# Head norms in the two mixers on 8 columns, in a four-layer decoder trunk on one core

## The chip, the cores and the metric

One core of a Trainium2 chip. The metric is the device time of one execution in microseconds (us), median of several runs; lower is better. PE is TensorE (PEld its weight loads), DVE VectorE, ACT ScalarE, POOL GpSimd, SP the queue that issues DMAs.

## The reference

The program is a trunk of residual layers on 512 positions of 1024 channels. Each layer is a SwiGLU FFN, a mixer, and another FFN. Layer 0's mixer (mixer A) is a recurrent one with 12 heads of 64 channels, together with a cross-attention of 4 heads to a memory of 256 rows. Layer 1's mixer (mixer B) is a dilated sliding-window attention of 12 heads, with the same kind of memory attention. What matters here are norms over the 64 channels of a head, at each position:

```
kk = split_heads(k * kk_scale)
kk = kk / jnp.maximum(jnp.linalg.norm(kk, axis=-1, keepdims=True), 1e-12)
...
y = ((y - mean) * lax.rsqrt(var + LNX_EPS)).reshape(b, s, RWKV_W) * lnx_g + lnx_b
...
q = rms_norm(q, q_gain)          # queries of the memory and of the dilated attention
k = rms_norm(split_heads(k), k_gain)
logits = jnp.einsum('bshd,bmhd->bhsm', q, k).astype(jnp.float32) / math.sqrt(HEAD_DIM)
```

## The kernel before

Activations lie transposed: 128 channels (two heads, a "pair") on the partitions, 512 positions in the free dimension, eight such tiles for 1024 channels. Products with weights (`dense`, L416) split each f32 operand into a high and a low part and make three matmuls of 512 columns in place of one f32 matmul, which would be slower; the weights' parts are made by ACT (`whi`) and by DVE or POOL (`wlo`), in the mixers by POOL alone. All else on PE is plain f32, in two records for each matmul in the trace, or a transpose by the identity.

Mixer A (`mixer_a`) projects six pairs of recurrent heads and two pairs of memory queries. For each pair `rwkv_prepare` makes the decays, the normed kk and the scaled operands, `rwkv_solve` inverts triangular blocks in steps that alternate between PE and DVE (tiles `tx` and `TT`, 32x32 matmuls), and `rwkv_finish` carries the state through eight chunks and norms the output. Mixer B (`mixer_b`) projects 8 query, 6 key and 6 value tiles; `settle` norms or transposes each, `dilated` makes the attention in 8 units of 128 positions and one pair, and `memory_attention` (used by both mixers) is called for each of the memory's two pairs.

A head's norm (`head_norm`) squares the tile on ACT, sums the squares with one f32 matmul against `same`, a 128x128 matrix of ones in two diagonal blocks, so that each channel of the head holds the sum, takes the root on ACT, inverts 128x512 numbers on DVE in four reciprocals of 128 columns (`invert`), and multiplies tile, gain and inverse on DVE. All 64 rows of a head hold the same number. `rwkv_prepare` and `rwkv_finish` do the same in their own code, with a floor of 1e-12 for kk. There are 28 such norms: in mixer A 6 of kk, 6 of the output and 2 of memory queries, in mixer B 6 of keys and 8 of queries (6 dilated, 2 memory). Four more, of the memory's keys, run on 256 columns in the FFNs.

What sets the order: the mixers are generators ("strands") woven by `weave`, which keeps a planner's clock for each engine (`Meter`) and at each point resumes the first strand in its list whose last result is due; projections come near the end of the list and so fill the gaps. The instructions then stand in that fixed order in each engine's queue. The recording helper is one line, L292, so groups are told apart by tile: `tmp` are work tiles, `krv` a pair's k, r, v, `sc`, `mm`, `py` and `fps` banks of PSUM (`sc` has four), `cst` the constants (`same`, the identity and the masks), `qn` and `kh` queries and keys of mixer B, `prob` its logits, `mpr` the memory's probabilities, `rstd` the layer norm's factor.

## Time and profile before

| | |
|---|---|
| median of three runs | 2133.26 us (2132.96 to 2133.29) |
| profiled execution, its time | 2133.8 us |
| its span | 2131.9 us |
| mean granted PE clock | 0.983 |
| busy | PE 97%, PEld 77%, DVE 46%, ACT 38%, POOL 28% |
| mixer A, about | 385 to 775 us |
| mixer B, about | 1538 to 1773 us |

A row of groups reads: line, engine, operation, out<-in, shapes, count | busy us, mean ns of one | idle time of the engine just before them and what ended most of it. PE's records overlap, so the mean of one matmul is longer than the distance to the next. A row of the chain of waits is a start, a duration in us, an engine and a tile. The clock of a row by stretch is the share of full speed that PE was granted.

### The profile page before, as it was taken

What the parts mean: (1) busy time and instruction counts of PE and PEld (TensorE: products, weight loads), DVE (VectorE), ACT (ScalarE), POOL (GpSimd) and SP (SyncE); (2) the same over time, 40 slices, a digit from 0 to 9 for tenths busy, and PEclk for the clock granted to TensorE, in tenths of its full rate; (3) what the DMA queues carried; (4) which work ended last, traced back from release to release, by engine and by line L of the source; (5) the groups of instructions that cost most, each with busy time, mean ns of one, the idle gap of its engine ahead of it and who ended that gap; (6) DMA issues with size and microseconds to landing.
All of it is one profiled execution on the core that took longest, in us unless ns stands there. A gap on an engine that the chain in (4) does not pass through costs nothing.

```text
span 2131.9 us, 35298 instructions
## 1 busy us (share of the span) xinstructions
PE 2057.6 (97%) x14270; PEld 1642.0 (77%) x14270; DVE 971.3 (46%) x1354; ACT 818.1 (38%) x1418; POOL 593.2 (28%) x514
## 2 busy tenths in 40 slices
PE   8999999979888899999999999999999999999999
PEld 6888888857665678788888888888777667888887
DVE  6333343564748556333434533333367675333322
ACT  6333333423334554333433433333336454333321
POOL 2222222643433143222222222222242224222221
PEclk9999999989999899999999999999999899999999
DMA  5333344411100064363344433334531044323342
GB/s 194 98 95 98 91 136 125 117 46 35 44 23 22 13 216 144 98 183 95 110 124 140 145 97 99 96 102 126 149 109 49 29 159 157 96 97 96 94 136 82
DMA packets 130644, 222.04 MB, mean 104 GB/s; under 512 B 14232, under 2 KB 31824, under 8 KB 130480
## 3 DMA queue, kind: packets, MB, share of 16 engines
q1 hardware_dynamic: 130480, 219.78, 33.6%
q8 instruction: 112, 1.84, 0.4%
q14 instruction: 52, 0.43, 0.1%
HBM read 202.84 MB, written 21.61 MB: 105 GB/s over the span
## 4 chain that ended last, share of the span: by engine, by line
PE 66%; DVE 5%; ACT 1%; POOL 1%; issue 1%; DVEq 0%; POOLq 0%
PE fps L292 51%; PE mm L292 7%; PE sc L292 6%; DVE tmp L292 2%; PE py L292 2%; DVE prob L292 1%; DVE tx L292 0%; DVE mpr L292 0%; DVE x L292 0%; DVE ul L292 0%; DVE krv L292 0%; ACT tmp L292 0%; ACT mpr L292 0%; POOL tmp L292 0%; DVE mx L292 0%
## 5 line engine op out<-in xcount | busy, mean ns | idle before, releaser
L292 POOL TENSOR_TENSOR wlo<-raw,whi 128x512 fp32r<-128x512 f32 (+3 forms) x404 | 495.3, 1227 | 1411.3 <-ACT whi L292 1402.4
L292 ACT ACTIVATE whi<-raw 128x512 fp32r<-128x512 f32 (+3 forms) x684 | 416.0, 610 | 943.3 <-PE fps L292 780.0
L292 PE MATMUL fps<-uh,whi 128*128 128x512 f32 x1408 | 551.4, 392 | 8.7 <-ACT whi L292 8.7
L292 PE MATMUL fps<-uh,wlo 128*128 128x512 f32 x1408 | 549.7, 391 | 2.4 <-DVE wlo L292 2.4
L292 PE MATMUL fps<-ul,whi 128*128 128x512 f32 x1408 | 548.9, 390 | 0.0
L292 DVE TENSOR_TENSOR wlo<-raw,whi 128x512 fp32r<-128x512 f32 x280 | 201.0, 718 | 346.5 <-ACT whi L292 336.9
L292 PEld LDWEIGHTS fps<-uh,whi 128*128 128x128 f32 x1408 | 264.9, 188 | 68.6 <-ACT whi L292 11.9
L292 PEld LDWEIGHTS fps<-uh,wlo 128*128 128x128 f32 x1408 | 264.9, 188 | 59.8 <-DVE wlo L292 4.0
L292 PEld LDWEIGHTS fps<-ul,whi 128*128 128x128 f32 x1408 | 264.9, 188 | 55.4 <-issue 0.7
L292 PE MATMUL fps<-hh,whi 128*128 128x512 f32 x704 | 273.9, 389 | 0.0
L292 PE MATMUL fps<-hl,whi 128*128 128x512 f32 x704 | 273.9, 389 | 0.0
L292 PE MATMUL fps<-hh,wlo 128*128 128x512 f32 x704 | 273.9, 389 | 0.0
L292 DVE TENSOR_TENSOR gs<-fps,rstd 128x512 f32<-128x512 f32 x88 | 60.5, 690 | 322.8 <-PE fps L292 322.8
L292 PEld LDWEIGHTS fps<-hl,whi 128*128 128x128 f32 x704 | 132.1, 188 | 27.5
L292 PEld LDWEIGHTS fps<-hh,whi 128*128 128x128 f32 x704 | 132.1, 188 | 27.4
L292 PEld LDWEIGHTS fps<-hh,wlo 128*128 128x128 f32 x704 | 132.1, 188 | 27.4
L292 PE MATMUL mm<-uh,whi 128*128 128x512 f32 x280 | 123.1, 440 | 0.5 <-DVE p L292 0.2
L292 DVE TENSOR_TENSOR hm<-fps,gs 128x512 f32<-128x512 f32 x88 | 60.6, 691 | 120.3 <-PE fps L292 115.8
L292 PE MATMUL mm<-ul,whi 128*128 128x512 f32 x280 | 115.2, 411 | 0.0
L292 PE MATMUL mm<-uh,wlo 128*128 128x512 f32 x280 | 114.2, 408 | 0.0
L292 DVE RECIPROCAL tmp<-tmp 128x128 f32<-128x128 f32 x112 | 97.2, 916 | 22.5 <-ACT tmp L292 22.1
L292 DVE TENSOR_TENSOR hl<-hm,hh 128x512 fp32r<-128x512 f32 x88 | 77.0, 877 | 51.0 <-ACT hh L292 51.0
(262 smaller groups left out, 2093.5 us busy)
## 6 DMA issues: line engine op xcount, KB each, us to landing
raw<-w SPq DMA_DIRECT2D x512, 256.0 KB, 2.6
raw<-wa_in SPq DMA_DIRECT2D x44, 256.0 KB, 2.7
xd<-x SPq DMA_DIRECT2D x40, 256.0 KB, 3.9
tmp<-xd SPq DMA_DIRECT2D x32, 256.0 KB, 3.6
xin<-xd SPq DMA_DIRECT2D x32, 256.0 KB, 4.2
raw<-w_kv SPq DMA_DIRECT2D x24, 256.0 KB, 2.7
raw<-w SPq DMA_DIRECT2D x32, 128.0 KB, 2.3
raw<-wmem SPq DMA_DIRECT2D x16, 256.0 KB, 2.6
```

What stands on the lines that cost most here:

```text
L292: r = f(*args, **kw)
```

## The change

The sum of squares is now taken by position and head. For each block of 128 positions the squared tile is the stationary side of a matmul, and `pair`, two columns of `same` (one per head), the moving side: positions lie on the partitions, and the four blocks and two heads make 8 columns. Scaling, epsilon (or the floor, now on the square), reciprocal and root run there (`roots`), the reciprocal before the root. Then there are two ways.

- Wide (18 norms: kk, output, keys of mixer B): the root writes each number 64 times, and `spread` multiplies the result with the identity, which brings it back to channels by positions in PSUM, from where the product reads it.
- Narrow (10 norms, all of queries): the tile stays as it is. The factor of a position and head goes into the logits, where positions lie on the partitions: as a scalar in the addition of the bias in `dilated`, and in the maximum and the scale of the exponential in `memory_attention`. The query's gain and 1/8 are folded into the keys' gain, once, at the program's start.

The memory's keys keep the old form (`wide=False`), with the folded gain. The diff, cut to its core:

```diff
+        self.gains = self.cp.tile([P, 3], F32, name="gains")
+        for i, (q, k) in enumerate(GAINS):
+            nc.vector.tensor_scalar(self.gains[:, i:i + 1], self.v(q), self.v(k), 0.125, op0=ALU.mult, op1=ALU.mult)
...
+        self.pair = self.same.rearrange("p (e u) -> p e u", e=2)[:, :, 0]
...
+    def head_rms(self, t, n, tmp, bank, wide=False):
+        sq = tmp()
+        self.nc.scalar.activation(sq, t, AF.Square)
+        yield WAIT
+        return (yield from self.roots(sq, n, bank, tmp if wide else None, 1.0 / HD, EPS, ALU.mult, ALU.add))
+
+    def roots(self, sq, n, bank, wide, *change):
+        nc, nb = self.nc, n // P
+        ps = bank("sc")[:, :nb * 2].rearrange("p (b e) -> p b e", e=2)
+        for b in range(nb):
+            nc.tensor.matmul(ps[:, b], sq[:, b * P:(b + 1) * P], self.pair, start=True, stop=True,
+                             skip_group_check=True)
+        r = self.xp.tile([P, 4, 2], F32, tag="roots", bufs=ROOTS, name=self.nm("roots"))[:, :nb]
+        nc.vector.tensor_scalar(r, ps, *change[:2], **{f"op{i}": o for i, o in enumerate(change[2:])})
+        nc.vector.reciprocal(r, r)
+        yield WAIT
+        if wide:
+            w = wide().rearrange("p (b e u) -> p b e u", e=2, u=HD)
+            nc.scalar.activation(w, r.unsqueeze(3).broadcast_to([P, nb, 2, HD]), AF.Sqrt)
+            r = w.rearrange("p b e u -> p b (e u)")
+        else:
+            nc.scalar.activation(r, r, AF.Sqrt)
+        yield WAIT
+        return r
+
+    def spread(self, r, ps):
+        for b in range(r.shape[1]):
+            self.nc.tensor.matmul(ps[:, b * P:(b + 1) * P], r[:, b], self.ident, start=True, stop=True,
+                                  skip_group_check=True)
...
-            nc.vector.tensor_scalar(mx, mx, -0.125, None, op0=ALU.mult)
+            rh = r[:, 2 * h:2 * h + 2].rearrange("p i e -> p e i")
+            nc.vector.scalar_tensor_tensor(mx, mx, -1.0, rh, op0=ALU.mult, op1=ALU.mult)
...
-                    nc.scalar.activation(pr[e][:, i], lg[e][:, i], AF.Exp, bias=mx[:, e, i:i + 1], scale=0.125,
+                    nc.scalar.activation(pr[e][:, i], lg[e][:, i], AF.Exp, bias=mx[:, e, i:i + 1], scale=rh[:, e, i:i + 1],
...
-        ss = self.bank("sc")
-        pe.matmul(ss, self.same, sq, start=True, stop=True)
-        inv = sq
-        act.activation(inv, ss, AF.Sqrt)
-        yield WAIT
-        vec.tensor_scalar(inv, inv, 1e-12, None, op0=ALU.max)
-        yield from self.invert(inv)
-        kk = inv
+        root = yield from self.roots(sq, T, self.bank, self.tmp, 1e-24, None, ALU.max)
+        inv = self.bank("sc")
+        self.spread(root, inv)
+        kk = sq
...
-                        nc.vector.tensor_tensor(s[:, e, 4:], ps[e], bias[:, 2 * m + e, 7:], op=ALU.add)
+                        for g in range(2):
+                            nc.vector.scalar_tensor_tensor(s[:, e, 4 + g], ps[e][:, g],
+                                                           rq[2 * (g + 1) + m][:, t, e:e + 1],
+                                                           bias[:, 2 * m + e, 7 + g], op0=ALU.mult, op1=ALU.add)
```

The planner draws a new order for both mixers. Three places, with the helper's line L292 before and L295 after. First DVE in mixer A, late in the solve of the fifth pair (`tx`, `TT`), beside the kk norm of the sixth. Before, and then after:

```order
L292 STREAM_TRANSPOSE tx_7030<-TT_6823 128x256
L292 TENSOR_TENSOR tx_7066<-sc_7033,cst 128x256
L292 TENSOR_SCALAR tmp_6948<-tmp_6948 128x512
L292 RECIPROCAL tmp_6948<-tmp_6948 128x128
L292 TENSOR_TENSOR TT_6823<-TT_6823,sc_7071 128x256
L292 RECIPROCAL tmp_6948<-tmp_6948 128x128
L292 STREAM_TRANSPOSE tx_7107<-TT_6823 128x256
L292 RECIPROCAL tmp_6948<-tmp_6948 128x128 x2
L292 TENSOR_TENSOR tx_7143<-sc_7110,cst 128x256
L292 SCALAR_TENSOR_TENSOR tmp_6948<-krv_6247,kks_3200,tmp_6948 128x512
```
```order
L295 TENSOR_TENSOR tx_7141<-sc_7108,cst 128x256
L295 TENSOR_TENSOR ul_8089<-y_3605,uh_8088 128x512
L295 TENSOR_TENSOR TT_6761<-TT_6761,sc_7154 128x256
L295 TENSOR_SCALAR roots_7198<-sc_7193 128x8
L295 STREAM_TRANSPOSE tx_7206<-TT_6761 128x256
L295 RECIPROCAL roots_7198<-roots_7198 128x8
L295 TENSOR_SCALAR roots_7215<-sc_7210 128x8
L295 TENSOR_TENSOR ul_8091<-y_4691,uh_8090 128x512
L295 RECIPROCAL roots_7215<-roots_7215 128x8
L295 TENSOR_TENSOR ul_8093<-y_5478,uh_8092 128x512
L295 TENSOR_TENSOR ul_8095<-y_6265,uh_8094 128x512
L295 SCALAR_TENSOR_TENSOR tmp_7101<-krv_6359,kks_3202,sc_7223 128x512
```

The floor and four reciprocals stood between the solve's steps; two steps on 8 columns stand there now, a second pair (`roots_7215`, a memory query's norm) among them, and the product reads PSUM (`sc`).

Second PE at the end of the same solve, before and after (`mm` are projection matmuls):

```order
L292 MATMUL mm_8201<-ul_8034,whi_8234 128x512
L292 MATMUL mm_8201<-uh_8033,wlo_8235 128x512
L292 MATMUL sc_7110<-tx_7107,mb_6797 32x32 x32
L292 MATMUL sc_7146<-TT_6823,tx_7143 32x32 x32
L292 MATMUL sc_7189<-tx_7181,mb_6797 32x32 x16
L292 MATMUL sc_7211<-TT_6823,tx_7206 32x32
L292 MATMUL sc_7233<-cst,AR_6683 128x128 x4
```
```order
L295 MATMUL mm_7144<-ul_2768,whi_7259 128x512
L295 MATMUL mm_7144<-uh_2767,wlo_7260 128x512
L295 MATMUL mm_7144<-uh_2883,whi_7259 128x512
L295 MATMUL sc_7223<-cst,tmp_7218 128x128 x4
L295 MATMUL sc_7229<-tx_7206,mb_6726 32x32 x16
L295 MATMUL mm_7144<-ul_2884,whi_7259 128x512
L295 MATMUL mm_7144<-uh_2883,wlo_7260 128x512
L295 MATMUL mm_7144<-uh_2999,whi_7259 128x512
```

Before, the solve's last steps follow each other with nothing between; now projection matmuls and the spread (`sc<-cst,tmp 128x128 x4`) stand between them.

Third PE in mixer B, after, at the norm of the first key tile:

```order
L295 MATMUL sc_14938<-cst,tmp_14930 128x2 x4
L295 MATMUL mm_14920<-kvh_12336,whi_14923 128x512
L295 MATMUL mm_14920<-kvl_12337,whi_14923 128x512
L295 MATMUL mm_14920<-kvh_12336,wlo_14924 128x512
L295 MATMUL mm_14920<-kvh_12425,whi_14951 128x512
L295 MATMUL mm_14920<-kvl_12426,whi_14951 128x512
L295 MATMUL mm_14920<-kvh_12425,wlo_14952 128x512
L295 MATMUL sc_14960<-cst,tmp_14958 128x128 x4
```

Where one sum over 512 columns stood in the stream of projections, there are now four of 2 columns, six projection matmuls, and the spread.

More of the change, by code (lines that the diff above doesn't have):

```diff
@@ L135, in pack @@
         at[f"gmem{l}"] = col(mem_norm[l])
+    at["gkv"] = col(kv_norm)
+    for l in range(2):
         at[f"mq{l}"], at[f"mk{l}"] = col(np.tile(mem_q_norm[l], 2)), col(np.tile(mem_k_norm[l], 2))
-    at["gkv"] = col(kv_norm)
     at["kvk"], at["bq"] = col(np.tile(kv_k_norm, 2)), col(np.tile(b_q_norm[0], 2))
@@ L222, in rstd @@
         return r
+ROOTS = 12
 WAIT, FREE = "wait", "free"
@@ L390, in load_constants, with gain @@
             off += w
+        self.pair = self.same.rearrange("p (e u) -> p e u", e=2)[:, :, 0]
+    def gain(self, i):
+        return self.gains[:, i:i + 1]
     def v(self, name, j=0):
@@ L529, in memory_kv @@
             if j < 2:
-                yield from self.head_norm(kh[:, j], t, self.v(f"mk{layer}"), tmp, bank, MEM)
+                yield from self.head_norm(kh[:, j], t, self.gain(layer), tmp, bank, MEM, wide=False)
             else:
@@ L537, in memory_kv, with head_norm @@
                 yield FREE
-    def head_norm(self, out, t, gain, tmp, bank, n):
-        nc = self.nc
+    def head_rms(self, t, n, tmp, bank, wide=False):
[25 more added lines that the diff above has]
+                                  skip_group_check=True)
+    def head_norm(self, out, t, gain, tmp, bank, n, wide=True):
+        nc = self.nc
+        if wide:
+            r = yield from self.head_rms(t, n, tmp, bank, True)
+            ps = bank("sc")[:, :n]
+            self.spread(r, ps)
+            nc.vector.scalar_tensor_tensor(out, t, gain, ps, op0=ALU.mult, op1=ALU.mult)
+            yield WAIT
+            return
         sq = tmp()
@@ L548, in head_norm, with memory_attention @@
         yield WAIT
-        yield from self.invert(sq)
+        for c in range(0, n, P):
+            nc.vector.reciprocal(sq[:, c:c + P], sq[:, c:c + P])
+            yield WAIT
         nc.vector.scalar_tensor_tensor(out, t, gain, sq, op0=ALU.mult, op1=ALU.mult)
         yield WAIT
-    def invert(self, t):
-        for c in range(0, t.shape[-1], P):
-            self.nc.vector.reciprocal(t[:, c:c + P], t[:, c:c + P])
-            yield WAIT
-    def memory_attention(self, j, q, kv, pool, bank, out):
+    def memory_attention(self, j, q, r, kv, pool, bank, out):
         nc = self.nc
@@ L682, in memory @@
                 yield from until(lambda: len(q) > j)
-                yield from self.head_norm(om[j], q[j], self.v("mq0"), self.tmp, bank, T)
+                r = yield from self.head_rms(q[j], T, self.tmp, bank)
                 yield from until(lambda: self.made[NPAIR - 1])
-                yield from self.memory_attention(j, om[j], kv, pool, bank, om[j])
+                yield from self.memory_attention(j, q[j], r, kv, pool, bank, om[j])
             def spare():
@@ L1009, in rwkv_finish @@
         yield WAIT
+        root = yield from self.roots(sq, T, self.bank, self.tmp, 1.0 / HD, LNX_EPS, ALU.mult, ALU.add)
         var = self.bank("sc")
-        pe.matmul(var, self.same, sq, start=True, stop=True)
-        act.activation(sq, var, AF.Sqrt, bias=self.epsx, scale=1.0 / HD)
-        yield WAIT
-        yield from self.invert(sq)
-        vec.scalar_tensor_tensor(y0, y0, self.v("lg", j), sq, op0=ALU.mult, op1=ALU.mult)
+        self.spread(root, var)
+        vec.scalar_tensor_tensor(y0, y0, self.v("lg", j), var, op0=ALU.mult, op1=ALU.mult)
         yield WAIT
@@ L1082, in mixer_b @@
                                                       ap=[[36 * 256 - 1, P], [256, 9], [1, P]]))
-            gain = pool.tile([P, 1], F32, name="qgain")
-            nc.vector.tensor_scalar(gain, self.v("bq"), 0.125, None, op0=ALU.mult)
             kh = pool.tile([P, 6, T], F32, name="kh")
@@ L1098, in project @@
                     yield step
-                t = q[m] if kind == "q" and m >= 6 else self.tmp()
+                t = q[m] if kind == "q" else self.tmp()
                 nc.vector.tensor_tensor(t, ps, rr[0] if kind == "q" else rkv, op=ALU.mult)
@@ L1126, in settle @@
                     elif kind == "k":
-                        yield from self.head_norm(kh[:, m], t, self.v("kvk"), self.tmp, bank, T)
-                    elif m < 6:
-                        yield from self.head_norm(q[m], t, gain, self.tmp, bank, T)
+                        yield from self.head_norm(kh[:, m], t, self.gain(2), self.tmp, bank, T)
+                    else:
+                        rq[m] = yield from self.head_rms(t, T, self.tmp, bank)
                     done.add((kind, m))
@@ L1142, in dilated @@
                     for e in range(2):
-                        nc.vector.tensor_tensor(s[:, e, :4], ps[e].rearrange("p (k u) -> p k u", u=P),
-                                                bias[:, 2 * m + e, 3 - t:7 - t], op=ALU.add)
+                        nc.vector.scalar_tensor_tensor(s[:, e, :4], ps[e].rearrange("p (k u) -> p k u", u=P),
+                                                       rq[m][:, t, e:e + 1], bias[:, 2 * m + e, 3 - t:7 - t],
+                                                       op0=ALU.mult, op1=ALU.add)
                     ps = [bank("sc", (P, 2, P)) for _ in range(2)]
@@ L1195, in memory @@
                     yield from until(lambda: ("q", 6 + j) in done)
-                    qs = self.tmp()
-                    yield from self.head_norm(qs, q[6 + j], self.v("mq1"), self.tmp, bank, T)
-                    yield from self.memory_attention(j, qs, kv, pool, bank, om[2 + j])
+                    yield from self.memory_attention(j, q[6 + j], rq[6 + j], kv, pool, bank, om[2 + j])
                     remembered.append(j)
```

6 lines of the change are left out of this document (2 added, 4 removed).

## The prediction

> **What bounds the kernel now.** I read the page first: the span, the busy line, the slices and the chain that ended last.
>
> ```profile
> span 2131.9 us, 35298 instructions
> ...
> PE 2057.6 (97%) x14270; PEld 1642.0 (77%) x14270; DVE 971.3 (46%) x1354; ACT 818.1 (38%) x1418; POOL 593.2 (28%) x514
> ...
> PE   8999999979888899999999999999999999999999
> ...
> PE 66%; DVE 5%; ACT 1%; POOL 1%; issue 1%; DVEq 0%; POOLq 0%
> ```
>
> TensorE (PE) is busy 97% of the span and carries 66% of the chain. In the slices it is at 9 nearly everywhere: the four FFNs and the projections are a stream of matmuls, and nothing outside PE counts there. The slices below 9 lie in the recurrent mixer A. So the second view was the busy time by stretch. Each row gives the stretch, its length, the busy time of PE, weight loads, DVE (VectorE), ACT (ScalarE) and POOL, the granted PE clock, the DMA share and GB/s. The first three rows are mixer A, the last four mixer B.
>
> ```profile
> 385.00:656.00 271.00, 243.21 (x4368) 174.86 (x4366) 161.99 (x240) 94.88 (x169) 119.87 (x123) 0.95 0.15 45
> 656.00:698.00 42.00, 32.39 (x731) 22.38 (x733) 36.60 (x57) 17.00 (x28) 13.29 (x12) 0.90 0.06 20
> 698.00:775.00 77.00, 68.25 (x1404) 49.69 (x1402) 40.10 (x83) 38.29 (x93) 11.84 (x13) 0.92 0.20 62
> 1538.00:1590.00 52.00, 50.79 (x213) 39.26 (x212) 38.32 (x44) 21.19 (x34) 21.22 (x17) 1.00 0.45 135
> 1590.00:1660.00 70.00, 68.06 (x419) 50.53 (x418) 47.95 (x75) 38.60 (x80) 17.95 (x14) 1.00 0.16 51
> 1660.00:1692.00 32.00, 27.32 (x89) 16.59 (x88) 15.16 (x25) 16.70 (x34) 4.72 (x4) 0.73 0.08 25
> 1692.00:1760.00 68.00, 63.30 (x375) 47.80 (x374) 51.78 (x78) 34.88 (x71) 17.84 (x20) 1.00 0.42 136
> ```
>
> Mixer A (390 us) leaves PE idle for 27.8 + 9.6 + 8.8 = 46 us, and the clock falls short of 1.00 by 0.05 x 271 + 0.10 x 42 + 0.08 x 77 = 24 us of full-speed time. From 656 to 698 DVE is busy 36.6 of 42 us (87%). In mixer B the four rows give 1.2 + 1.9 + 4.7 + 4.7 = 12.5 us idle, and 0.27 x 32 = 8.6 us of clock, all of that in one place. The two mixers together thus hold about 90 us that a change of this kind could reach. Third, what PE waited for in mixer A (engine and tile, releaser; total, times, longest), and the reciprocals of the norms in its stretches (first 385:656, then 656:698, then 385:775).
>
> ```profile
> PE sc L292 <- DVE tx L292: 24.0, 19, 2.6
> PE sc L292 <- DVE tmp L292: 8.2, 3, 5.5
> ```
> ```profile
> L292 DVE RECIPROCAL tmp<-tmp 128x128 f32<-128x128 f32 x32 | 28.0, 918 | 1.3 <-ACT tmp L292 1.2
> ```
> ```profile
> L292 DVE RECIPROCAL tmp<-tmp 128x128 f32<-128x128 f32 x16 | 14.1, 918 | 0.1
> ```
> ```profile
> L292 DVE RECIPROCAL tmp<-tmp 128x128 f32<-128x128 f32 x56 | 49.1, 918 | 1.6 <-ACT tmp L292 1.4
> ```
>
> 32 of the 46 us end on DVE: on `tx`, the small steps of the triangular solve, and on `tmp`. Of DVE's work in mixer A, 49.1 us are the 56 reciprocals of 14 norms, in the same queue as the solve.
>
> **The prices.** From the groups with shapes kept apart (count, busy us, mean ns of one, idle before):
>
> ```profile
> L292 DVE RECIPROCAL tmp<-tmp 128x128 f32<-128x128 f32 x112 | 97.2, 916 | 22.5 <-ACT tmp L292 22.1
> ...
> L292 DVE TENSOR_TENSOR prob<-sc,bias 128x512 f32<-128x512 f32 x16 | 10.3, 682 | 8.8 <-PE sc L292 8.8
> ...
> L292 DVE SCALAR_TENSOR_TENSOR tmp<-tmp,vec,tmp 128x512 f32<-128x512 f32 x6 | 7.5, 1258 | 0.0
> ...
> L292 DVE TENSOR_SCALAR tmp<-tmp 128x512 f32<-128x512 f32 x12 | 6.0, 500 | 8.1 <-ACT tmp L292 8.1
> ...
> L292 DVE TENSOR_TENSOR prob<-sc,bias 128x256 f32<-128x256 f32 x16 | 6.0, 415 | 0.0
> L292 DVE SCALAR_TENSOR_TENSOR qn<-tmp,qgain,tmp 128x512 f32<-128x512 f32 x6 | 5.9, 980 | 0.1
> ...
> L292 DVE SCALAR_TENSOR_TENSOR tmp<-krv,kks,tmp 128x512 f32<-128x512 f32 x6 | 5.4, 905 | 0.1
> ...
> L292 DVE SCALAR_TENSOR_TENSOR tmp<-sc,tmp 128x512 f32<-128x512 f32 x6 | 4.1, 678 | 11.1 <-PE sc L292 11.1
> ...
> L292 DVE RECIPROCAL sm<-sm 128x4 f32<-128x4 f32 x8 | 1.3, 165 | 10.6 <-ACT mpr L292 8.2 <-ACT krv L292 2.2
> L292 DVE TENSOR_SCALAR mx<-mx 128x4 f32<-128x4 f32 x8 | 1.3, 161 | 0.2
> ```
> ```profile
> L292 ACT ACT_TABLE_LOAD x41 | 52.6, 1283 | 5.4 <-DVE mx L292 2.4 <-PE sc L292 1.7 <-PEq L1291 0.7
> ...
> L292 ACT ACTIVATE tmp<-tmp 128x512 f32<-128x512 f32 x24 | 14.9, 627 | 15.3 <-DVE tmp L292 15.3
> ...
> L292 ACT ACTIVATE tmp<-sc,eps 128x512 f32<-128x512 f32 x16 | 11.0, 689 | 24.1 <-PE sc L292 23.9
> ...
> L292 ACT ACTIVATE warm<-eps 128x1 f32<-128x1 f32 x1 | 0.2, 202 | 0.0
> ```
>
> *DVE.* All 28 norms lose four reciprocals, 4 x 0.918 = 3.67 us, and get a scaling from PSUM and a reciprocal on 8 columns. The nearest rows, on 4 columns, are 0.161 and 0.165, so 0.33 us together; below by nothing, above by the 0.415 that 256 columns from PSUM take, so 0.83. I take 0.33, by the rows nearest in size. The 18 wide norms (6 kk, 6 of the recurrent output, 6 k) keep their product, now with PSUM as one operand: 0.68 by the row `tmp<-sc,tmp`, where 0.905 (kk) and 1.258 (the output) stood; for k I count no gain. The kk norms also lose the floor, 0.50. The 10 query norms lose the product (0.98 for six). In the dilated units 16 additions of 512 columns keep their size (0.68); 16 of 256 become 32 of 128. By the rows 0.682 and 0.415 a column is 1.04 ns, so 128 columns are an estimated 0.28: 32 x 0.28 - 16 x 0.415 = +2.3 us. In all DVE loses some 110 us of 971.
>
> *ACT.* A wide root stays at 0.63 (was 0.69), a narrow one is about 0.2. This is small, and lies beside PE.
>
> *PE.* The price is read from the chain in mixer B and from two rows of loads.
>
> ```profile
> 1550.77 0.86 PE sc L292 x2
> 1551.63 5.24 PE mm L292 x23
> ```
> ```profile
> 560.82 0.42 PEld L292 LDWEIGHTS sc<-cst,beta 128*128 128x128 f32 x4 [0.17 <-DVE mb L292]
> ```
> ```profile
> L292 PE MATMUL sc<-cst,beta 128*128 128x128 f32 x24 | 3.9, 286 | 1.8 <-DVE mb L292 1.8
> ```
>
> The old sum is one 512-column f32 matmul in two records, 0.86 us on the chain; a projection matmul is 5.24 / 23 = 0.228. The new sum is four matmuls of 2 columns, each with its own 128x128 load, and since an f32 matmul is two records, eight loads. No row shows this. Four 128x128 loads of transposes stand without a gap in 0.42 us, so eight are 0.84. Below, all eight could vanish under the stream around them: 0. Above, none of a record's 0.286 is hidden: 8 x 0.286 = 2.3. I take 0.84, by the row with the same load. The spread by the identity streams 512 f32 columns like the old sum: 0.86. So a query norm changes PE by nothing, a wide one adds 0.84: 12 x 0.84 = 10.1 in mixer A, 6 x 0.84 = 5.0 in mixer B. With the ends the total for both mixers is -10 x 0.86 = -9 to 18 x 2.3 + 10 x 1.44 = +56.
> [...]
>
> **The sum.** What a shorter DVE queue gives is not its time, but the part that something waits for. I take as that part DVE's busy share of the stretch, since only a queue with work behind the reciprocal hands its time on.
> - Mixer A, reciprocals out: 28.0 x 0.60 + 14.1 x 0.87 + 7.0 x 0.52 = 16.8 + 12.3 + 3.6 = -32.7.
> - New small steps there: 14 x 0.33 x 0.67 = +3.1 (0.67 = 32.7 / 49.1, the mean share).
> - Floor and cheaper products: (6 x 0.50 + 6 x 0.23 + 6 x 0.58 + 2 x 1.2) x 0.67 = -6.9, the last being the products of the two query norms, by the row 1.258.
> - PE's 10.1 us more, at PE's share 344 / 390 = 0.88: +8.9.
> - PE now waits for ACT's root before each spread: 12 x 0.25 = +3, a choice near the lower end; the upper one is rival 3.
> - Mixer B, the place where a norm stands bare:
>
> ```profile
> 1676.94 0.70 ACT tmp L292
> 1677.66 3.39 DVE tmp L292 x4
> ...
> 1683.26 6.41 PE sc L292 x18
> ```
> ```profile
> 1538.62 0.14 DVE qgain L292
> ```
>
> Root and four reciprocals stand on the chain, 0.70 + 3.39, against 0.17 + 0.17 + 0.2 after: -3.5. Here PE ran at half clock, 18 records in 6.41 us. In the new order 25 projection matmuls stand behind the sum, so I give back half of the 8.6 us: -4.3. What is late next here is the softmax of the memory heads, which stays.
> - The query gain at the mixer's start, now made at the program's start: -0.1. Of the other 7.8 us idle in mixer B (1.2 + 1.9 + 4.7) a quarter, a choice, since softmax steps and not norms stand before most of it: -2. Elsewhere PE's stream hides the DVE savings wholly.
> - PE's 5.0 us more, all on the path: +4.9 with the query norms. The 32 smaller additions: +1. In the new order six matmuls, 6 x 0.228 = 1.37 us, stand between sum and spread, and the way through them is 0.17 + 0.17 + 0.63 and four hand-overs that I take at 0.1 (a choice): +1 for six.
>
> The cover is the projection stream; where a spread comes without it, the way costs its whole 1.4 us, which the +3 of mixer A stands for. Together: mixer A -24.6, mixer B -3.0, **-28 us**. The profiled execution took 2133.8 us (span 2131.9), 0.5 above the median 2133.26: 2133.8 - 28 - 0.5 = **2105 us**.
>
> How idle time and clock hang together, two rows show: 6 us in mixer A after a late DVE step, and the next 6.
>
> ```profile
> 434.00:440.00 6.00, 1.61 (x3) 0.84 (x3) 4.26 (x4) 0.00 (x0) 2.76 (x3) 0.72 0.14 44
> 440.00:446.00 6.00, 5.91 (x72) 3.08 (x70) 2.95 (x5) 3.79 (x5) 2.58 (x3) 0.71 0.15 45
> ```
>
> PE is busy 1.6 of 6 us, and the clock falls to 0.72 and stays at 0.71 in the next 6. [...]
>
> **The rivals.**
> 1. *The whole loss comes back.* If the reciprocals cause both the idle time and the clock's fall, 46 + 24 + 8.6 + 5 go, less PE's 15: -68, 2065 us. For it: 32 of 46 us wait on DVE. Against: the solve is a chain of PE and DVE steps that alternate, and that stays. Halfway between it and the forecast is -48, 2085 us.
> 2. *The chain of the solve is the bound, not DVE's queue.* Then only the saturated 42 us and the bare norm pay: -12.3 - 7.8 - 0.1, and PE's 13.8 and the waits 5 come on top: -1, about 2132. For it: outside 656 to 698 DVE is only 52 to 60% busy.
> 3. *PE waits at the spread* (slower than before). In the old norm only DVE waited for the root; now PE's queue does, in order, with the solve and the projections behind it, 18 times. In mixer A a table load (1.28 us) stands ahead of each kk root, and two weight copies of 0.63 can be queued before it: 1.28 + 1.26 = 2.5 us for each spread, 18 x 2.5 = 45, 2105 + 45 = 2150 us. It decides from 28 / 18 = 1.6 us a spread beyond what I counted. Against: the order puts 3 to 12 matmuls between sum and spread, and the load needs no data. The same end is reached if the small matmuls take 2.3 us (56 - 15 = +41).
> 4. *The change doesn't do what it says*: the order is drawn by a planner whose prices are its own, and a bad draw may undo part. I see none: in the rows of the order shown with the change, the solve's steps have projection matmuls between them where they had none. It widens the range by some 10 us either way.
>
> **The chances.** Forecast (-12 to -45): 0.58. Rival 1 (-45 to -70): 0.12, of it 0.02 below 2070. Rival 2 (-12 to +4, of which 0.08 within 0.2%): 0.19. Rival 3 with the bad draw: 0.11. A measurement of this kernel tells 0.2% (4.3 us) from no change. So faster 0.58 + 0.12 + 0.11 = 0.81, same 0.08, slower 0.11. The range holds the forecast, most of rival 1 (0.10) and the part of rival 2 that gains at least 3 us (0.13), 0.81 in all: 2070 to 2130.
>
> **What would show it.** Right, if mixer A from its start to the first matmul of the next FFN is some 25 us shorter, with DVE clearly under 80% in every 40 us of it, PE's waits for `tx` and `tmp` under 20 us, and if PE's waits for the wide roots stay under 1 us each. If four small matmuls take much over 0.84 us, the PE term is wrong; if PE waits for ACT on the spread, rival 3 holds; if the waits for `tx` stay near 24 us, rival 2. Mixer B should keep its length within some 8 us, without the half-clock stretch. It would be wrong, above all, if the share rule for the DVE queue is wrong: it is the largest term and a choice.

## The result, and the profile after

The changed kernel took 2118.82 us in the median of 5 runs (2117.79 to 2124.02), the kernel before 2133.29 (2132.96 to 2133.56). The ratio is 0.994, with a 95% interval of 0.9924 to 0.9955: 14.5 us faster by the medians and 12.8 by the means, on which the ratio rests: about half of the 28 that were forecast, and inside the range. The profiled execution of the changed kernel took 2117.79 us, the least of the five, and is 16.0 us shorter than the profiled one before (2133.8).

The page of the changed kernel, its span, its busy line and PE by slices:

```profile
span 2116.0 us, 35895 instructions
...
PE 2068.4 (98%) x14582; PEld 1662.6 (79%) x14582; DVE 872.1 (41%) x1300; ACT 813.3 (38%) x1416; POOL 587.7 (28%) x513
...
PE   8999999989999999999999999999999999999999
```

DVE lost 99 us of 971, as the change intends, and the slices of mixer A are nearly full. Yet PE, which was the bound, is busy 11 us longer than before. To see where, the execution is cut into its stages. A stage begins with the first matmul of its kind in the timeline: `mm<-uh` for a mixer, `fps<-uh` for the first product of an FFN, `fps<-hh` for its second. For mixer A of the changed kernel (start, us, engine, names, shapes):

```profile
388.31 0.48 PE L295 MATMUL mm<-uh,whi 128*128 128x512 f32 x1
...
778.00 0.40 PE L295 MATMUL fps<-uh,whi 128*128 128x512 f32 x1
```

All ten stages, read in this way from both profiles (us):

| stage | before | after | difference |
|---|---|---|---|
| FFN 00, first product | 247.1 | 246.4 | -0.8 |
| FFN 00, second product and memory keys | 132.4 | 135.8 | +3.4 |
| mixer A | 413.2 | 389.7 | -23.5 |
| FFN 01, first | 259.3 | 261.3 | +2.0 |
| FFN 01, second | 119.7 | 123.2 | +3.5 |
| FFN 10, first | 240.3 | 240.3 | 0 |
| FFN 10, second | 119.7 | 123.2 | +3.5 |
| mixer B | 226.5 | 220.9 | -5.6 |
| FFN 11, first | 243.3 | 241.2 | -2.1 |
| FFN 11, second, to the end | 124.3 | 127.9 | +3.6 |

The prediction looked at mixer A up to 775 us, 24 us short of its end at 798.9; there PE is never idle, so the 46 us that it counted as idle are those of the whole mixer. The mixers gave 29.1 us, close to the forecast's 27.6. But each of the four second products, on which no line of the diff works, lost 3.5 us, 14 in all. That is where half of the gain went. The second product of FFN 10 by stretch, first before and then after (columns as in the prediction's table of stretches):

```profile
1418.13:1537.81 119.68, 119.68 (x530) 99.10 (x528) 41.54 (x51) 37.18 (x63) 28.58 (x26) 1.00 0.43 126
```
```profile
1402.81:1526.01 123.20, 123.20 (x530) 99.12 (x529) 41.52 (x51) 37.27 (x63) 28.61 (x26) 1.00 0.42 123
```

The same 528 matmuls (two more records reach over the edges), the same weight loads, DVE, ACT and POOL within 0.1 us, the clock at 1.00 in both, PE never idle. Only the matmuls stand further apart: 119.68 / 528 = 0.2267 us before, 123.20 / 528 = 0.2333 after. The groups of the page say the same, for all four FFNs (count, busy us, mean ns), before and after:

```profile
L292 PE MATMUL fps<-hh,whi 128*128 128x512 f32 x704 | 273.9, 389 | 0.0
```
```profile
L295 PE MATMUL fps<-hh,whi 128*128 128x512 f32 x704 | 278.1, 395 | 0.0
```

In the mixers themselves nearly all the signs that the prediction asked for are there. DVE is busy at most 62% of any 40 us of mixer A (24.6 us, from 668 to 708). PE's waits in mixer A of the changed kernel (total, times, longest):

```profile
PE sc L295 <- DVE tx L295: 12.8, 8, 2.9
...
PE sc L295 <- DVE tmp L295: 2.4, 1, 2.4
...
PE sc L295 <- ACT tmp L295: 1.6, 4, 0.6
```

`tx` and `tmp` are down from 32 to 15 us, and the roots that PE now waits for cost 1.6 us in all. The mixers by stretch, before and after:

```profile
385.70:798.90 413.20, 367.05 (x6597) 265.63 (x6596) 253.06 (x396) 163.80 (x315) 161.07 (x160) 0.94 0.20 60
1537.80:1764.30 226.50, 213.97 (x1112) 157.93 (x1111) 157.51 (x222) 115.31 (x224) 66.12 (x57) 0.96 0.31 96
```
```profile
388.30:778.00 389.70, 362.88 (x6777) 277.09 (x6776) 204.09 (x360) 160.21 (x312) 154.68 (x160) 0.98 0.21 64
1526.00:1746.90 220.90, 214.40 (x1243) 168.11 (x1242) 105.68 (x201) 113.22 (x224) 66.08 (x57) 0.99 0.31 97
```

PE's idle time in mixer A fell from 46.2 to 26.8 us. Of mixer B's 0.04 x 226.5 = 9 us of lost clock, 0.01 x 220.9 = 2 are left. So two questions were open: what slows matmuls that nobody changed, and whether the mixers' agreement is what it looks like.

### The profile page after: what moved, and what is told of

Its sections match the earlier page's. It is cut to its first block, busy times and chain, and to the rows that moved or that the text cites. A ratio compares the mean times of both kernels' runs of the same rounds, so it can differ in the third digit from the quotient of the medians.

```text
span 2116.0 us, 35895 instructions
## 1 busy us (share of the span) xinstructions
PE 2068.4 (98%) x14582; PEld 1662.6 (79%) x14582; DVE 872.1 (41%) x1300; ACT 813.3 (38%) x1416; POOL 587.7 (28%) x513
## 5 line engine op out<-in xcount | busy, mean ns | idle before, releaser
L295 POOL TENSOR_TENSOR wlo<-raw,whi 128x512 fp32r<-128x512 f32 (+3 forms) x404 | 494.5, 1225 | 1422.7 <-ACT whi L295 1412.2
L295 ACT ACTIVATE whi<-raw 128x512 fp32r<-128x512 f32 (+3 forms) x684 | 416.2, 610 | 938.9 <-PE fps L295 792.3
L295 PE MATMUL fps<-uh,whi 128*128 128x512 f32 x1408 | 551.6, 392 | 7.6 <-ACT whi L295 7.6
L295 PE MATMUL fps<-uh,wlo 128*128 128x512 f32 x1408 | 549.7, 390 | 2.1 <-POOL wlo L295 1.8
L295 PE MATMUL fps<-ul,whi 128*128 128x512 f32 x1408 | 548.9, 390 | 0.0
L295 DVE TENSOR_TENSOR wlo<-raw,whi 128x512 fp32r<-128x512 f32 x280 | 201.8, 721 | 355.4 <-ACT whi L295 346.4
L295 PEld LDWEIGHTS fps<-uh,whi 128*128 128x128 f32 x1408 | 264.8, 188 | 67.7 <-ACT whi L295 11.2
L295 PEld LDWEIGHTS fps<-uh,wlo 128*128 128x128 f32 x1408 | 264.8, 188 | 60.2 <-POOL wlo L295 3.9
L295 PEld LDWEIGHTS fps<-ul,whi 128*128 128x128 f32 x1408 | 264.9, 188 | 55.8 <-issue 0.7
L295 PE MATMUL fps<-hh,wlo 128*128 128x512 f32 x704 | 278.1, 395 | 0.0
L295 PE MATMUL fps<-hh,whi 128*128 128x512 f32 x704 | 278.1, 395 | 0.0
L295 PE MATMUL fps<-hl,whi 128*128 128x512 f32 x704 | 278.1, 395 | 0.0
L295 DVE TENSOR_TENSOR gs<-fps,rstd 128x512 f32<-128x512 f32 x88 | 60.5, 690 | 322.9 <-PE fps L295 322.9
L295 PEld LDWEIGHTS fps<-hh,wlo 128*128 128x128 f32 x704 | 132.2, 188 | 32.2
L295 PEld LDWEIGHTS fps<-hl,whi 128*128 128x128 f32 x704 | 132.2, 188 | 32.1
L295 PEld LDWEIGHTS fps<-hh,whi 128*128 128x128 f32 x704 | 132.2, 188 | 31.9
L295 PE MATMUL mm<-uh,whi 128*128 128x512 f32 x280 | 123.0, 439 | 1.0 <-DVE x L295 0.7
L295 PE MATMUL mm<-ul,whi 128*128 128x512 f32 x280 | 113.2, 404 | 0.0
L295 PE MATMUL mm<-uh,wlo 128*128 128x512 f32 x280 | 112.3, 401 | 0.0
L295 DVE TENSOR_TENSOR hm<-fps,gs 128x512 f32<-128x512 f32 x88 | 60.6, 691 | 121.2 <-PE fps L295 115.4
L295 DVE TENSOR_TENSOR hl<-hm,hh 128x512 fp32r<-128x512 f32 x88 | 77.2, 880 | 51.1 <-ACT hh L295 51.0
L295 PEld LDWEIGHTS mm<-uh,whi 128*128 128x128 f32 x280 | 53.2, 190 | 17.5 <-issue 4.6
```

The costliest lines, as they stand in the source:

```text
L295: r = f(*args, **kw)
```

## Experiments: where the tiles lie

The changed kernel draws 12 small tiles for its roots (`roots`, 8 f32 numbers, 32 B a partition each) from the state pool. The pools lie in SBUF, the on-chip memory, one behind the other, so everything behind the state pool starts 12 x 32 = 384 B later. In the built programs (bytes in a partition, first tile of each):

```
            before   changed   roots_in_mixers
whi          18080     18080     18080
uh           34464     34464     34464
hh (FFN 00)  97952     98336     97952
hl (FFN 00) 143008    143392    143008
```

Before, `hh` and `hl` lie a whole number of 2048 B from the weights `whi`, and `uh` does in both. Theory "place": this distance sets the pace of the matmuls.

**The roots elsewhere, nothing else changed.** The instructions and their order are the same in both programs:

```diff
-        r = self.xp.tile([P, 4, 2], F32, tag="roots", ...
+        r = self.pool.tile([P, 4, 2], F32, tag="roots", ...
```


> The changed kernel with one word changed: the small tiles of the roots (12 of 32 B a partition) come from the mixer's own pool, not from the state pool. In the changed kernel they lie last in the state pool, so every pool behind it starts 384 B later in SBUF than before, the FFN's hh and hl with it. Theory 'place': the matmuls of the FFN's second product went from 0.2267 to 0.2328 us apart because hh and hl lie 384 B further on, while the weights stayed. Then the four second products fall back to 0.2267 us and lose what they had gained, about 3.5 us each, and the kernel takes 2118.8 - 14 = 2105 us (2101 to 2109), mixers as in the changed kernel. Rival 'work': they are slower because the engines beside them run another order of work, or the instructions lie elsewhere; then 0.2328 us stays and the time is 2116 to 2124. Rival 'chip': the two profiles came from chips of different speed; then nothing is settled by the place and the spacing is the same in all runs of this call.

Measured: 2110.12 us (5 runs, 2103.97 to 2111.91), ratio to before 0.9879 (0.986 to 0.9899). All four second products are back; that of FFN 10:

```profile
1398.75:1518.44 119.69, 119.69 (x530) 99.14 (x529) 41.54 (x51) 37.18 (x63) 28.63 (x26) 1.00 0.43 126
```

Profile against profile, the span went from 2116.0 to 2103.9: 12.1 us less: the four second products give 14.0, and mixer A took 1.7 us more in this execution (391.4). The median lies 5 us above the expected 2105 and just outside its band; the runs here, those of before too (2127.45 to 2139.16), scatter more than the first five did.

**The shift alone, in the kernel before.** No instruction differs:

```diff
+            self.xp.tile([P, 96], F32, name="pad")
             pool = ctx.enter_context(tc.tile_pool(name="mixa", ...
```


> The kernel before with a tile of 384 B a partition, never written or read, at the end of the state pool: no instruction differs, every pool behind starts 384 B later, as in the changed kernel. Theory 'place': matmuls of the second products 0.2328 us apart instead of 0.2267, four times 3.5 us, 2133.3 + 14 = 2147 us (2143 to 2151), mixers and first products unchanged to 1 us. Rivals 'work' and 'chip': 2133 us, 0.2267.

Measured: 2149.82 us (6 runs, 2146.05 to 2156.64), ratio 1.0079 (1.0059 to 1.01). Mixer A took 413.3 us, as before; the group of the page is that of the changed kernel:

```profile
L292 PE MATMUL fps<-hh,wlo 128*128 128x512 f32 x704 | 278.1, 395 | 0.0
```

An unused tile alone costs what the changed kernel lost. "Work" and "chip" fall.

**The shift for the weights too.**

```diff
         nc.gpsimd.memset(self.epsx, LNX_EPS)
+        self.cp.tile([P, 96], F32, name="pad")
```


> The kernel before with the same unused 384 B in the pool of the constants, which lies first: weights, uh and ul, and hh and hl all move by 384 B, so that the weights and the moving operand keep their distance. If what counts is the distance of the moving tile from the weight tile (the distance modulo their 2048 B was 0 before, and is 384 after), all products stay at 0.2267 us: 2133 us (2129 to 2137). If what counts is where the moving tile itself starts, the second products go to 0.2328 and the first products, whose uh and ul move as well, do the same: 4 x 3.5 + 4 x 6.5 = 40 us more in the FFNs and some 8 in the mixers' projections, 2173 to 2181 us. Rivals 'work' and 'chip': 2133, which this run alone would not tell from the first.

Measured: 2134.13 us (10 runs, 2130.55 to 2140.21), ratio 1.0 (0.9987 to 1.0013), the second products at 0.2267 us (119.68 / 528), the records of the first ones at 390 to 392 ns in the mean, as before. It is not where the moving tile starts, but how far it lies from the tiles ahead of it, of which the second product reads the weights.

**Other distances.** A tile of another size in each FFN, ahead of `hh`:

```diff
+                if m == 0 and PADS[which]:
+                    hp.tile([P, PADS[which] // 4], F32, bufs=1, ...)
                 hh = hp.tile([P, T], F32R, tag="hh", bufs=NF, ...)
```


> The kernel before with an unused tile ahead of hh in each FFN's pool, of another size in each of the four: 32, 64, 128 and 256 B. Theory 'place': the spacing of the second product's matmuls depends on the size, between 0.2267 and 0.233 us or beyond; if the rule is one of alignment to 64 B only the first differs, if it is distance modulo a larger block it grows with the size or appears from one on. Rivals: 0.2267 in all four.

> The kernel before with the unused tile ahead of hh in each FFN's pool again, now of 96, 160, 192 and 224 B. The spacings so far, by the distance of hh from the weights: 0 B 0.2267 us, 32 B 0.2333, 64 B 0.2289, 128 B 0.2333, 256 B 0.2267, 384 B 0.2333. Theory 'place', with a block of 256 B (384 acts as 128, 256 as 0): all four of these lie off the block's start and are slower than 0.2267, the odd multiples of 32 B at 0.2333 as 32 B is, 192 B between 0.2267 and 0.2333. Should one of them be faster than 0.2267, that distance would pay in all products of the FFNs. Rival: no block of 256 B, and some of them are at 0.2267 as well.

The second products by stretch in the first of the two (the rows follow the program: 32, 64, 128 and 256 B):

```profile
253.52:376.72 123.20, 123.20 (x529) 98.95 (x528) 42.91 (x53) 37.20 (x63) 26.57 (x24) 1.00 0.42 123
1061.86:1182.73 120.87, 120.87 (x529) 99.16 (x528) 45.93 (x53) 37.20 (x63) 26.67 (x24) 1.00 0.44 127
1423.07:1546.26 123.19, 123.19 (x529) 99.11 (x528) 41.55 (x51) 37.32 (x63) 28.60 (x26) 1.00 0.42 123
2011.74:2131.42 119.68, 119.68 (x529) 98.91 (x527) 33.22 (x38) 27.36 (x46) 25.31 (x23) 1.00 0.37 109
```

and in the second (96, 160, 192, 224 B; the last row lacks nine records of 528, so its pace is 121.10 / 519):

```profile
253.99:377.20 123.21, 123.21 (x529) 99.11 (x528) 42.82 (x53) 37.21 (x63) 26.58 (x24) 1.00 0.41 123
1062.16:1185.85 123.69, 123.69 (x529) 99.45 (x528) 45.94 (x53) 37.22 (x63) 26.60 (x24) 1.00 0.42 124
1426.13:1549.32 123.19, 123.19 (x529) 98.74 (x528) 41.46 (x51) 37.22 (x63) 28.47 (x26) 1.00 0.41 123
2019.10:2140.20 121.10, 121.10 (x520) 97.49 (x519) 33.10 (x38) 27.36 (x46) 25.18 (x23) 1.00 0.36 108
```

0.2267 us at 0 and 256 B, 0.2289 at 64, 0.2333 to 0.2343 at 32, 96, 128, 160, 192, 224 and 384. That 192 B would lie between was a miss. A block of 256 B fits all ten values, of which only 256 and 384 test that it repeats; no distance is faster than the old one. Each value but 0 and 384 was seen in one FFN only.

## Experiments: what the mixers' terms are worth

**The largest term alone.** The reciprocals of the norms are left out of the kernel before, which then computes other numbers:

```diff
-            self.nc.vector.reciprocal(t[:, c:c + P], t[:, c:c + P])
+            c = t[:, c:c + P]
+            self.nc.meter.note("vector", "reciprocal", (c, c), {})
...
-        act.activation(inv, ss, AF.Sqrt)
+        act.activation(inv, ss, AF.Sqrt, scale=1e-20)
```


> The kernel before without the 112 + 4 reciprocals of its norms (their results are not inverted, and the root of kk is taken of 1e-20 of the sum so that nothing overflows); the planner is told of their time all the same, so the order moves little. It measures the prediction's largest term alone: 'a DVE queue that is shorter gives its share'. Theory of the prediction: mixer A 413.2 - 32.7 = 380.5 us (377 to 384), mixer B some 4 to 8 us less than its 226.5, FFNs unchanged at 0.2267, in all about 2096 us. Rival 1 (the whole loss comes back): mixer A 343 us. Rival 2 (the chain of the solve is the bound): mixer A about 400 us.

Measured: 2105.92 us (one run). The mixers:

```profile
386.10:780.00 393.90, 359.65 (x6597) 262.32 (x6596) 198.60 (x336) 163.57 (x315) 156.95 (x160) 0.97 0.19 64
1518.90:1736.50 217.60, 207.09 (x1112) 155.62 (x1111) 109.39 (x166) 114.94 (x224) 66.08 (x57) 0.99 0.31 100
```

Mixer A lost 19.3 us, not 32.7, for 49.1 us less of DVE: a share of 0.39 where the rule had 0.67. So taking the reciprocals out and putting nothing in their place gives *less* in mixer A than the whole change, which adds PE work on top. Something else was at work in the changed kernel; the order of the work was the candidate. It was not held here either: PE's sequence of tiles in mixer A departs from that of before about as far as in the redraw at 0.19 below, which by itself made mixer A 6 us shorter.

The same without the line that tells the planner of the missing reciprocals:

> As 'no_recip' (reciprocals of the norms left out, results not inverted), but the planner knows that they are gone and draws the order anew. 'no_recip' gave mixer A 393.9 us, 19.3 less than before, where the prediction's rule wanted 32.7. If an order that suits the shorter DVE queue matters, mixer A falls to 380 to 386, about the 32.7 of the rule; if DVE's time alone counts, it stays at 391 to 397; if the draw is chance, anything, and then 'draw_before' shows moves of the same size.

Measured: 2100.95 us, mixer A 392.6, mixer B 214.7. In mixer A the new order gave 1.3 us more, in the band that was set for "DVE's time alone counts". Against the mean of the five orders of the kernel before that are drawn below (408.4), the two orders without reciprocals gave 14.5 and 15.8 us, a share of 0.30 to 0.32.

**Twice the new small matmuls,** on top of `roots_in_mixers`:

```diff
+            for _ in range(2):
                 nc.tensor.matmul(ps[:, b], sq[:, b * P:(b + 1) * P], self.pair, ...)
```


> The kernel 'roots_in_mixers' with each small matmul of the new sums issued twice (the second writes the same numbers again): 14 x 4 more in mixer A, 14 x 4 in mixer B. It measures what the new PE work costs. In the trace of the changed kernel a sum of four takes PE 0.81 to 0.98 us. By the prediction's rule (PE's share, 0.88 in mixer A, and all of it in mixer B) mixer A goes from 391 to 391 + 0.88 x 14 x 0.92 = 402 us, mixer B from 220 to 220 + 14 x 0.85 = 232 us. If the small matmuls mostly fill PE's idle time: mixer A under 395. If they cost more by what they hold up behind them: over 406.

Measured: 2154.82 us, mixer A 422.7 (+31.3), mixer B 239.4 (+19.4); far over "over 406". The planner drew another order for it, so the same again with the second matmul hidden from the planner:

> As 'sums_twice', but the planner is not told of the second small matmuls, so that the order of the work stays that of 'roots_in_mixers' but for a few places. 'sums_twice' lengthened mixer A by 31 us (391.4 to 422.7) and mixer B by 19 (220.0 to 239.4), where PE's own time for the added matmuls is 14 x 0.92 = 12.9 and 14 x 0.85 = 11.9. Theory 'price': PE's time counts by its share, so now mixer A 402 us, mixer B 232, and the rest of the 31 and 19 was the other order drawn. Rival 'chain': the small matmuls stand in a chain that ends late and cost more than their time; then mixer A stays above 412.

Measured: 2149.49 us. The mixers:

```profile
385.20:802.50 417.30, 391.63 (x6890) 302.80 (x6888) 203.04 (x359) 160.09 (x311) 154.71 (x160) 0.93 0.18 59
1543.70:1782.00 238.30, 230.83 (x1356) 185.03 (x1355) 107.13 (x201) 113.28 (x224) 65.87 (x57) 0.96 0.29 91
```

Mixer A is 25.9 us longer than the 391.4 of `roots_in_mixers`, for 12.9 us of matmuls; mixer B 18.3 for 11.9. That is over the 412 that "chain" asked for, but not by its mechanism. PE's idle time in A stays at 25.7 (26.8 there). PE's busy time grew by 391.63 - 364.64 = 27.0, and the clock fell from 0.97 to 0.93, 0.04 x 417 = 17 us. So it is not waits that double the price, as "chain" had it, but matmuls at a lower clock. The trace shows where it falls. In the traces of the kernel before and of the changed one the granted clock is 1.00 or 0.50, and the stretches at 0.50 in the mixers last 3.41, 6.83, 10.24 or 13.65 us. Two stretches of 3.4 us at full clock in `sums_twice_kept`, one in each mixer, each with the stretch at half clock that follows:

```profile
501.00:504.40 3.40, 3.40 (x85) 2.92 (x83) 1.46 (x4) 0.93 (x2) 1.02 (x2) 1.00 0.21 77
504.40:507.80 3.40, 3.40 (x75) 3.03 (x74) 1.18 (x3) 0.03 (x1) 0.00 (x0) 0.50 0.03 7
1692.20:1695.60 3.40, 3.40 (x27) 3.18 (x27) 0.37 (x2) 0.95 (x3) 0.92 (x1) 1.00 0.26 95
1695.60:1702.40 6.80, 6.80 (x26) 6.21 (x27) 1.16 (x4) 1.87 (x3) 1.27 (x1) 0.50 0.05 17
```

PE is busy all the time before the clock falls; 16 and 22 of its records there are sums with 2 columns. All 20 profiles were read in this way over 3.4 us, the shortest of those stretches, ahead of each fall in the mixers. In the eleven without the new sums PE was never busy for more than 75% of that time (0 to 56% ahead of the ten falls of the kernel before). In the nine with them 14 falls follow more than 80%, and each of the 14 has 8 to 24 of the narrow records in it; four of them are in kernels that issue the sums once (two in `k_old_form`, one each in `draw2_changed` and `draw3_changed`). That the narrow matmuls bring the clock down is thus likely, and would be a cost of the change that the forecast lacks; no run varies their width alone, and other falls still follow idle time (in the changed kernel PE was busy for 0 to 49% of the 3.4 us ahead of its four).

**Only the useful half in mixer B.** There the wide norms of the keys add PE work, and the projections hide the reciprocals that they save. On top of `roots_in_mixers`:

```diff
-  self.head_norm(kh[:, m], t, self.gain(2), self.tmp, bank, T)
+  self.head_norm(kh[:, m], t, self.gain(2), self.tmp, bank, T, wide=False)
```


> The kernel 'roots_in_mixers' with the six k norms of mixer B in their old form (one sum by the matrix of ones, root and reciprocals on 512 columns); the queries there and all of mixer A as changed. PE loses 6 x 0.84 = 5 us in mixer B and DVE gets back 6 x 3.3 us, of which PE waits for little, since the projections' stream stands behind. By the prediction's terms (PE +4.9, waits at the spread +1) mixer B is 5 to 6 us shorter than in 'roots_in_mixers', and the kernel at 2110 - 5 = 2105 us, with 2099 where the runs of the same kernel gave 2104. Rival: the reciprocals come back before the softmax steps and cost what they did, then the time is the same within 2 us or longer.

Measured: 2100.39 us (5 runs, 2095.64 to 2103.78), ratio to before 0.9837 (0.9822 to 0.9852): the lowest median of the study. Mixer B went from 220.0 to

```profile
1521.90:1735.50 213.60, 207.03 (x1159) 159.75 (x1158) 123.89 (x214) 113.92 (x224) 66.66 (x57) 0.99 0.32 101
```

which is 6.4 us less, all of it PE's (213.46 to 207.03), near the 5 to 6 that the forecast's terms for B give. The order in B is a new one here, and lengths of B move by as much with a draw alone (below); firmer is PE's busy time, which in five profiles of the changed mixer B at this clock of 0.99 lay between 212.8 and 214.4. Mixer A, in the same order as in the changed kernel and `roots_in_mixers` (389.7 and 391.4), took 394.6 in this execution: some 5 us is the spread of one order.

## Experiments: the draw

The order of the mixers' work comes from the planner, and any change of an instruction makes it draw anew. How much a draw is worth is measured by redrawing without changing an instruction, both kernels (the changed one with `roots_in_mixers`, so that the FFNs are alike):

```diff
-        late = end + 0.22
+        late = end + 0.25
```


> The kernel before with one constant of the planner changed (the time it allows after an instruction, 0.22 to 0.25): the same instructions, the mixers in another order. It measures how much of a mixer's length is the order drawn. If the draw counts little, mixer A stays at 413 and mixer B at 217 to 222 us, within 3. If it counts, they move by more than 5 us, and then a difference of 23.5 us between two kernels is not all due to their work.

> The kernel 'roots_in_mixers' with the same constant of the planner changed: the same instructions in another order. Mixer A was 391.4 us, mixer B 220.0. Same reading: within 3 us if the draw counts little, else more than 5. The difference of the two redrawn kernels is a second measurement of what the change gives in the mixers: the prediction's terms say -24.6 in mixer A and -3 in mixer B.

Mixer A of the two, 410.8 and 414.4 us (the rows are rounded at their ends):

```profile
385.70:796.60 410.90, 364.57 (x6598) 261.85 (x6597) 252.03 (x396) 164.23 (x315) 156.47 (x160) 0.97 0.19 61
```
```profile
385.80:800.10 414.30, 376.90 (x6776) 285.04 (x6775) 206.86 (x360) 161.38 (x313) 156.92 (x160) 0.95 0.19 60
```

With the constant at 0.25 the change made mixer A slower, and the whole kernel too, 2120.20 to 2134.18. Three more pairs followed, at 0.19, 0.28 and 0.31.

> The kernel before with the planner's constant at 0.19: the same instructions in another order. So far mixer A and mixer B of the kernel before took 413.2 and 226.5 us (0.22), and 410.8 and 215.6 (0.25). Theory 'work' (the change is worth about -24.6 in A and -3 in B whatever the order, and the redrawn changed kernel was one bad draw): A 405 to 418. Theory 'draw' (the order moves each kernel by 10 us or more, and the change itself gives less than that): A anywhere from 390 to 420.

> The kernel 'roots_in_mixers' with the planner's constant at 0.19. So far 391.4 and 220.0 us (0.22), 414.3 and 227.6 (0.25). Theory 'work': A 385 to 397, some 20 to 25 under draw2_before. Theory 'draw': A anywhere from 385 to 420, on either side of draw2_before.

> The kernel before with the planner's constant at 0.28. Theory 'work': mixer A 405 to 418 us. Theory 'draw': 390 to 420.

> The kernel 'roots_in_mixers' with the planner's constant at 0.28. Theory 'work': mixer A 385 to 397 us, 20 to 25 under draw3_before. Theory 'draw': 385 to 420.

> The kernel before with the planner's constant at 0.31. Theory 'work': mixer A 405 to 418 us. Theory 'draw': 390 to 420.

> The kernel 'roots_in_mixers' with the planner's constant at 0.31. Theory 'work': mixer A 385 to 397 us, 20 to 25 under draw4_before. Theory 'draw': 385 to 420.

All pairs, one profiled execution each, in us; idle is the length less PE's busy time, time is that of the run. But for the first pair, the two of a pair ran on one chip, where the kernel before took 2132.26 to 2135.39. Of the kernel before with 0.22, mixer A was seen in five executions (with `pad384`, `pad_all384` and the two of other distances): 413.1 to 413.5. Mixer B took 222.2 to 227.2 in them, so that differences of 5 us say nothing in one pair.

| constant | A before | A changed | idle in A, before | changed | B before | B changed | time before | changed |
|---|---|---|---|---|---|---|---|---|
| 0.22 | 413.2 | 391.4 | 46.2 | 26.8 | 226.5 | 220.0 | 2133.80 | 2105.74 |
| 0.25 | 410.8 | 414.4 | 46.3 | 37.4 | 215.6 | 227.6 | 2120.20 | 2134.18 |
| 0.19 | 407.1 | 402.6 | 44.0 | 33.3 | 225.7 | 220.6 | 2127.17 | 2116.20 |
| 0.28 | 405.8 | 389.2 | 43.5 | 24.2 | 218.6 | 221.1 | 2117.57 | 2103.51 |
| 0.31 | 405.1 | 399.1 | 43.6 | 25.5 | 220.4 | 222.1 | 2119.90 | 2115.28 |

The differences in mixer A are -21.8, +3.6, -4.5, -16.6 and -6.0: a mean of -9.1 with a standard deviation of 10.1, so -9 +/- 13 at 95% with five pairs. In mixer B the mean is +0.9 +/- 9, and in the whole time -9 +/- 19. So five pairs don't show that the change gains anything whatever the order, even without the 14 us of the second products; what was measured at first is the gain of one pair of orders. The "work" theory, 20 to 25 us in A in each pair, fell with the first redraw and with each of the next three. The pair at 0.22, the one that the prediction speaks of, had of the five the longest mixer A before and the second shortest after. The pair with the fastest changed kernel, at 0.28, by stretch, before and changed:

```profile
385.20:791.00 405.80, 362.31 (x6597) 260.96 (x6595) 251.69 (x396) 165.04 (x315) 157.32 (x160) 0.97 0.19 61
```
```profile
385.70:774.90 389.20, 365.04 (x6777) 276.30 (x6776) 205.17 (x360) 160.45 (x312) 153.43 (x160) 0.98 0.21 64
```

What holds in every pair is the idle time: it falls by 19.4, 8.9, 10.8, 19.3 and 18.0 us, 15.3 +/- 6 in the mean. PE's busy time, lower clock included, moves by -2.4, +12.3, +6.3, +2.7 and +12.0, +6 +/- 8. The idle time is what the change gives in mixer A in all five orders; the rest is not told from the draw.

## Why the prediction was wrong

*The step that failed is the first one: in the FFNs "nothing outside PE counts there".* The sum had no term for them. True, PE streams there without a gap; but PE's own pace changed, by 0.0066 us x 528 x 4 = 14 us, through a pool that grew by 384 B. The ten stages add up: -29.1 in the mixers, +14.0 in the second products and -0.9 in the first ones are the 16.0 us between the two profiles. `pad384` shows it without the change, `roots_in_mixers` shows the change without it.

*Mixer A, -24.6 forecast, -23.5 measured: right by luck.* The reciprocals' term of -32.7 is too large: alone they gave -19.3 and -20.6 in two orders, against a kernel before whose order was the slowest of five. The rule that a shorter queue hands on its busy share overrates it; why it does is not shown. All DVE terms and waits together were put at -33.5 (-32.7 + 3.1 - 6.9 + 3), and the idle time over five draws fell by 15.3. PE's +8.9 agrees with +6 +/- 8. With -15.3 + 8.9 the sum would have been -6 and not -24.6; the five pairs measured -9 +/- 13. The two orders that happened to be compared made up the difference. Rival 4 named the bad draw and priced it at "some 10 us either way", and 10.1 is the measured standard deviation of the difference in A; the sentence "I see none" was wrong, since the rows of an order don't tell a good draw from a bad one.

*Mixer B, -3.0 forecast, -5.6 measured, +0.9 +/- 9 over the draws.* The PE term of +4.9 fits `k_old_form` (6.4 less of PE's busy time). The half-clock stretch, for which -4.3 stood, is not the norm's doing alone: in the kernel before with other distances (`phases1`, the same instructions) mixer B took 222.2 us instead of 226.5, with the clock at 0.98 instead of 0.96.

*The prices were nearly right.* The groups of the changed kernel, DVE and then ACT:

```profile
L295 DVE SCALAR_TENSOR_TENSOR prob<-sc,roots,bias 128x512 f32<-128x512 f32 x16 | 11.4, 747 | 12.5 <-PE sc L295 12.5
...
L295 DVE SCALAR_TENSOR_TENSOR prob<-sc,roots,bias 128x128 f32<-128x128 f32 x32 | 9.0, 343 | 0.0
...
L295 DVE RECIPROCAL roots<-roots 128x8 f32<-128x8 f32 x28 | 5.4, 194 | 0.6
L295 DVE TENSOR_SCALAR roots<-sc 128x8 f32<-128x8 f32 x28 | 4.6, 163 | 27.8 <-PE sc L295 27.7
```
```profile
L295 ACT ACTIVATE tmp<-roots 128x512 f32<-128x512 f32 x18 | 11.3, 630 | 21.3 <-DVE roots L295 21.2
```

The small steps take 0.163 + 0.194 = 0.36 us (0.33 forecast), the wide root 0.63 (0.63). The dilated units' additions cost +5.4 us instead of +2.3. Of the four small matmuls and the spread, the timeline of PE in mixer A:

```profile
666.98 0.95 PE L295 MATMUL sc<-cst,tmp 128*128 128x2 f32 x8
667.78 0.49 PE L295 MATMUL mm<-uh,whi 128*128 128x512 f32 x1
...
670.88 1.05 PE L295 MATMUL sc<-cst,tmp 128*128 128x128 f32 x8
671.86 0.31 PE L295 MATMUL sc<-tx,mb 32*32 32x32 f32 x8
```

From the start of one to the start of the next: 0.80 us for the sum (0.84 forecast; 0.80 to 0.98 over the 14 in mixer A, 0.92 in the mean), 0.98 for the spread (0.86 forecast; 1.00 in the mean there).

*The rivals.* Rival 1 falls: with no reciprocals at all mixer A keeps 34 us of idle time (393.9 - 359.65). Rival 2 lies nearer the truth than the forecast: it said that the solve's chain stays the bound, and of some 45 us idle the change takes 15 in the mean of the pairs; its -1 is nearer to the -9 of the five pairs than -28 is. Rival 3 falls: PE's waits for the wide roots are 1.6 us in mixer A, none longer than 0.6. A table load did run before its root's data were there: in the kernel before, the one at 449.30 us ended at 450.58, and the kk root behind it began at 454.98, after 4.40 us of waiting for PE's sum.

*What would show it* was nearly all seen, and it proved little: a shorter mixer A, less waiting for `tx`, a DVE under 80%, are also what a lucky draw looks like.

## What to carry to other kernels

Before a small tile goes into an early pool, see what moves behind it: in these FFNs a moving operand that kept its distance from the weights modulo 256 B kept PE's pace (0.2267 us, against 0.2289 to 0.2343 at the other distances), and the small tiles cost the second products nothing in a late pool (119.69 us in FFN 10, 119.68 before). Where a planner orders the work, one pair of kernels measures change and draw together; redraw both a few times before a difference is believed, and take the best draw at the end. And a shorter queue on a side engine gave PE back 0.3 to 0.4 of the time that it lost, less than its busy share (0.67 in the mean).
